# Hybrid decoder step: the first output block's gated rows prepared in the last projection round, rows loaded four halves deep, and three operations moved from GpSimd to VectorE

## The chip, the cores and the metric

The kernel runs on one core of one Trainium2 chip. The metric is the device time of one execution in microseconds (us), a median over runs. The engines are named as the profile names them: PE is TensorE's matmuls (PEld its weight loads), DVE is VectorE, ACT is ScalarE, POOL is GpSimd, and SP is the engine whose queue issues the DMAs.

## The reference, cut to what matters

Everything is float32. There are 1024 prompt rows and 8 samples of 4 rows, the model width is 1024, and there are two layers: one of sliding-window attention, then one of gated DeltaNet. The change lies nearly wholly in the second layer's output projection and in the samples' part of that layer.

```python
def modulate(x, c, norm_g, w_mod, b_mod):
    shift, scale, gate = jnp.split(jax.nn.silu(c) @ w_mod + b_mod, 3, axis=-1)
    h = rms_norm(x, norm_g) * (1 + scale[:, None]) + shift[:, None]
    return h, gate[:, None]
...
# each layer:  x <- x + gate * Branch(h);  a final rms_norm follows the last layer
# gated DeltaNet branch, per head (16 value heads of 128, chunks of 64 rows):
#   S_t = e^{g_t} S_{t-1} + k_t u_t^T
#   u_t = beta_t (v_t - (e^{g_t} S_{t-1})^T k_t),   o_t = S_t^T q_t / sqrt(dk)
#   out = (rms_norm(o) * silu(z)) @ w_out          # 2048 -> 1024
```

The samples start from states `S` that are loaded (one of 128 x 128 for each sample and head), and their new states are outputs.

## The kernel before, in words

Each fp32 matmul is made of three matmuls: an operand `x` is split into `hi` (a cast by ACT) and `lo` (a subtraction `x - hi` by DVE or POOL), and hi·hi, lo·hi and hi·lo are summed in PSUM.

The program is written out by a planner that runs when the kernel is built. Pieces of work are Python generators ("jobs"), which `weave(gen, name, hq)` hands over. A job yields a condition (`idle`, `sure`, `soon`, `over`, or a function) before it issues an instruction; the planner keeps a planned clock of each engine and picks among the waiting jobs by rank: the table `K`, in the closing stage (`nc.closing`) the table `KT`, and for the chains of head pair `hq` the table `KR`. `EX`, `TB`, `SW`, `MS` and `MM` are further numbers of the planner: margins and places. `GP` says which of five kinds of operation go to POOL instead of DVE. The engines run their instructions in the order that comes out; semaphores bind them.

On PE the program has these stages, by the time of the profiled execution: start to 74 us, attention layer to 394, its output projection to 508, DeltaNet's projections and chunk chains to 1348 (eight rounds, one for each pair of heads), and the closing stage to the end.

The closing stage multiplies the gated rows by `w_out`. `out_block(b)` makes block b of 18: part 0 (value heads 0 to 7) for eight blocks of 128 prompt rows and then the samples, and part 1 (heads 8 to 15) likewise. A block of prompt rows is 2 halves of the columns x 8 heads x 3 matmuls of 512 columns, and `pos[0]` counts 16 steps a block. Its jobs are:

- `prepare(b)` loads two halves of gated rows (`of`, 256 KB each, from the DRAM tile `gTd`), casts them (`ohi`, ACT) and subtracts (`olo`).
- `rows_of(b)` loads the rows `xt` to which the product is added.
- `gather(b)` multiplies the PSUM bank by the gate row (`y`, DVE), which frees the bank, and adds it to `xt`; `squares` and `finish` norm and store.
- `load_out` loads `w_out` in pieces of 128 x 512 (`wr`), casts them (`h2hi` or `whB`) and subtracts (`h2lo` or `wlB`).

Between the blocks' matmuls stand the last head pair's `chain` (matmuls `vo,UZ`, `uo,ks`, `S,qT`, `uo,DP`, `S,kT`), the gate row (`modG,selt`), and the samples: `states_times` multiplies the 128 loaded state tiles by the samples' queries and keys in `zq`, `core` does the recurrence, and `new_states` makes and stores the new states from `U` and `kb`.

Of the kernel before, what the change touches and what calls it, by code (L numbers as in the profile page):

```python
# [5 lines left out]
F32 = mybir.dt.float32  # L6
F32R = mybir.dt.float32r
# [7 lines left out]
P = 128  # L15
# [3 lines left out]
NB = TP // P  # L19
DB = 8  # L20
# [7 lines left out]
HQ = 8  # L28
# [214 lines left out]
def f(ap):  # L243
    return ap.bitcast(F32)
# [53 lines left out]
def body(tc, I, O, cst_ap, dbg=None):  # L298
# [19 lines left out]
    SP = (2, 20)  # L318
    AM = (3, 12)
    AT = (-5, 3)  # L320
    EX = (1.7, 2.5, 0.8, 0.7)
    ES, EN, EL, EM = EX
    K = {'split': 13, 'add': 0, 'attend': 40, 'turning': 0, 'modulate': 17, 'cached': 16, 'wo': 37, 'turn': 0, 'ahead': 2, 'taps': 2, 'gating': 5, 'decay': 23, 'samples': 38, 'load': 6, 'mod': 3, 'shape': 12, 'decays': 58, 'prepare': 58, 'gather': 8, 'finish': 10, 'states': 28, 'core': 2, 'new': 4}
    KT = {'prepare': 3, 'gather': 33, 'finish': 24, 'states': 19, 'core': 7, 'new': 14, 'load': 19, 'gating': 6, 'samples': 5, 'output': 23}
    KR = [{'chain': 4, 'output': 15, 'solve': 5, 'invert': 18, 'blocks': 40, 'decayed': 22}, {'chain': 31, 'output': 31, 'solve': 12, 'invert': 31, 'blocks': 39, 'decayed': 37}, {'chain': 9, 'output': 2, 'solve': 29, 'invert': 41, 'blocks': 1, 'decayed': 11}, {'chain': 23, 'output': 23, 'solve': 4, 'invert': 4, 'blocks': 0, 'decayed': 23}, {'chain': 10, 'output': 2, 'solve': 45, 'invert': 40, 'blocks': 1, 'decayed': 56}, {'chain': 8, 'output': 15, 'solve': 6, 'invert': 16, 'blocks': 49, 'decayed': 12}, {'chain': 0, 'output': 1, 'solve': 11, 'invert': 20, 'blocks': 34, 'decayed': 14}, {'chain': 10, 'output': 2, 'solve': 45, 'invert': 28, 'blocks': 1, 'decayed': 56}]
    TB = (3, 0)
    SW = (35, 1)
    MS = (39, 13)
    AH, AI = (a / 10 for a in AM)
    GP = (0, 1, 1, 1, 1)  # L330
    ORD = ['zzkv', 'zqzvk', 'zqzkv', 'qzzvk', 'qzzkv', 'vqzzk', 'qzzkv', 'qvzz']
    MM = (7, 12)
    ORDER = [("q", 2), ("q", 3), ("q", 4), ("q", 5), ("z", 0), ("k", 1), ("z", 1), ("z", 2), ("q", 6), ("q", 7),
             ("z", 3), ("z", 4), ("z", 5), ("z", 6), ("z", 7)]
    SE = ("vector", "vector", "vector", "vector")
# [213 lines left out]
    def over(*names):  # L549
        return lambda: not any(e[2] in names for e in jobs)  # L550
# [1333 lines left out]
    if True:  # L1884
# [446 lines left out]
        def load_out(*cuts):  # L2331
# [14 lines left out]
            while raws_:  # L2346
# [9 lines left out]
                loaded.add((k, hf))  # L2356
                fetch()

        def start():
            w_raw(0)  # L2360
            for q in range(2):
                yield idle("scalar", w_raw.tiles[0][q])
                w_split(0, q)
# [16 lines left out]
        for r in range(HQ):  # L2380
            if r > 0:
                weave(chain(r - 1, states.pop(r - 1)), "chain", r - 1)
                weave(decayed(r, states[r]), "decayed", r)
            pz = [2 * r, 2 * r + 1]
            for what in ORD[r]:
                if what in "kv" and r + 1 < HQ and r + 1 not in states:
                    states[r + 1] = {}
                    weave(decay_blocks(r + 1, states[r + 1]), "decay")
                    weave(solve(r + 1, states[r + 1]), "solve", r + 1)
                if what == "q":  # L2390
                    proj_kq(r, states[r], (1,))
                elif what == "z":
                    proj_z(pz.pop(0))
                elif what == "k":
                    until(lambda: finished[0] >= r - 1)
                    proj_kq(r + 1, states[r + 1], (0,))
                else:
                    until(lambda: gs is not None and gated[0] >= 4 * (r - 1))
                    proj_v(r, states[r])
                    if r + 1 == HQ:  # L2400
                        weave(chain(r, states.pop(r)), "chain", r)
# [11 lines left out]
        nc.parts |= {x2d.tensor.name, gTd.tensor.name}  # L2413
        gate = x3.tile([P, D], F32, name="gp", tag="gp")

        pos, prepared, stored, opened, gathered, outs = [0], {}, [0], [], [-1], [0]

        def prepare(b, part, t):

            cs = slice(t * P, (t + 1) * P)  # L2420
            ohl = prepared[b] = []
            if t == NB:
                yield over("core")
            for kk in range(2):
                if t == NB:
                    yield lambda: pos[0] >= 16 * (b - 1) + 8 + 8 * kk
                    gh = x3.tile([P, 4, P], F32R, tag="ohi", name="ohi", bufs=2)
                    g4 = gsT[:, HK * part + 4 * kk:HK * part + 4 * kk + 4]
                    yield idle("scalar", g4)
                    nc.scalar.copy(gh[:, :, 0:TS], g4)  # L2430
                    yield idle("vector", gh)
                    nc.vector.tensor_sub(gh[:, :, TS:2 * TS], g4, f(gh[:, :, 0:TS]))
                    ohl.append((gh,))
                    continue
                yield lambda: b == 0 or len(prepared[b - 1]) > kk
                r0 = part * HK + 4 * kk
                of = x3.tile([P, 4, P], F32, tag="of", name="of", bufs=2)
                nc.sync.dma_start(of, gTd[t, :, r0:r0 + 4])
                yield lambda: pos[0] >= 16 * (b - 1) + 8 + 8 * kk
                ohi = x3.tile([P, 4, P], F32R, tag="ohi", name="ohi", bufs=2)  # L2440
# [8 lines left out]
        xts_ = {}  # L2449

        def rows_of(b, part, t):
            yield lambda: stored[0] >= b - 1 - (b > NB)
            cs = slice(t * P, min((t + 1) * P, T))
            if b > NB and b % 3 == 0:
                xt = xts_[b] = hp.tile([P, D], F32, tag="h2lo2", name="xt")
            else:
                xt = xts_[b] = x3.tile([P, D], F32, tag="xt", name="xt", bufs=2)
            nc.sync.dma_start(xt[0:cs.stop - cs.start], (x2d if part else x1d)[cs])
# [80 lines left out]
        def out_block(b):  # L2539

            part, t = blocks_[b]
            for i in (0, 1) if b == 0 else (b + 1,):
                if i <= LB:
                    weave(prepare(i, *blocks_[i]), "prepare")
# [85 lines left out]
            convolved[half] = acc  # L2630

        def states_times():
            zq = sg.tile([P, DB, HQ, 32], F32, name="zq")
            yield from samples(0)
            qk = convolved[0].rearrange("p (i h) t -> p h i t", i=2)
            weave(samples(1), "samples")
# [13 lines left out]
            for b in range(DB):  # L2650
                yield idle("gpsimd")
                nc.gpsimd.memset(zq[:, b], 0.0)
            for b in range(DB):
                c0 = 8 * (b % 4)
                yield idle("vector", qk)
                nc.vector.tensor_copy(zq[:, b, :, c0:c0 + 8].rearrange("p h (i t) -> p h i t", i=2),
                                      qk[:, :, :, b * DS:(b + 1) * DS])
            ahead = 0
            for n in range(SB):
                if n == SB // 2:  # L2660
# [2 lines left out]
            for u in range(0, len(us_), 2):  # L2663
                b, hd, _ = us_[u]
                if u % 16 == 0:
                    yield over("chain", "output")
                    pk = yield from bank("mi")
                yield lambda: pos[0] >= SW[0] + SW[1] * (u + 1) / 10
                yield sure(ES, sts[u], sts[u + 1], zq)
                for j in range(4):  # L2670
                    nc.tensor.matmul(pk[32 * j:32 * j + 32, hd * 256:(hd + 1) * 256], zq[:, b, 4 * hd + j, :],
                                     sts[u + j // 2][:, 2 * (j % 2):2 * (j % 2) + 2, :].rearrange("p h d -> p (h d)"),
                                     start=(b % 4 == 0), stop=(b % 4 == 3), skip_group_check=True)
# [363 lines left out]
```

## Time and profile before

| what | value |
|---|---|
| median of 3 runs | 1617.11 us (1614.87 to 1619.9) |
| the profiled execution's own time | 1616.25 us |
| its span, first to last instruction | 1614.5 us |
| mean granted TensorE clock | 0.997 |
| PE busy | 1579.1 us |
| DVE busy | 1203.3 us |
| ACT busy | 843.1 us |
| POOL busy | 209.9 us |

The busy times are those of the span. In the profile's lines, `L84` is a helper that records nearly every operation, so instructions are told apart by their tiles: `ps_pj<-h2hi,olo` is the matmul that writes PSUM tile `ps_pj` from `h2hi` and `olo`. A line of waits has the engine and its tile, then the engine and the tile that it waited for, then total, count and the longest in us.

### The profile page before, as it was taken

How to read it: one execution, taken by the hardware profiler on the slowest of the kernel's cores; microseconds unless marked ns; L12 is line 12 of the kernel's file. 1: busy time of each engine (PE TensorE's matmuls, PEld its weight loads, DVE VectorE, ACT ScalarE, POOL GpSimd, SP SyncE). 2: the span in 40 equal slices, each digit the busy share in tenths (PEclk: the TensorE clock that was granted, in tenths of full speed). 3: DMA queues.
4: the chain of work that ended last, by engine and by line, in shares of the span. 5: the costliest groups of instructions: out<-in, count | busy, mean ns of one | idle time of the engine just before them, and what ended most of it. 6: DMA issues, size and time to landing. Idle time of an engine off the chain costs nothing. (4 is left out here: it accounts for less than half of the span.)

```text
span 1614.5 us, 30776 instructions
## 1 busy us (share of the span) xinstructions
PE 1579.1 (98%) x10714; PEld 1404.6 (87%) x10714; DVE 1203.3 (75%) x3781; ACT 843.1 (52%) x2422; POOL 209.9 (13%) x284
## 2 busy tenths in 40 slices
PE   9999999999999999999999999999999998999997
PEld 7888888987778999989999999999999997767775
DVE  6737677665665788897988769798688887757777
ACT  4635555444344655566564655665466465423332
POOL 1300000000223002020020000201001013233323
PEclk9999999999999999999999999999999999999999
DMA  9442220115343333233333324324243136675884
GB/s 365 153 140 79 79 81 28 40 47 154 103 146 108 98 93 81 81 92 91 105 70 90 100 58 128 72 62 121 65 126 80 46 102 206 202 263 178 289 270 158
DMA packets 178826, 195.70 MB, mean 121 GB/s; under 512 B 76848, under 2 KB 120720, under 8 KB 178640
## 3 DMA queue, kind: packets, MB, share of 16 engines
q1 hardware_dynamic: 178672, 193.75, 40.1%
q8 instruction: 84, 1.38, 0.4%
q14 instruction: 70, 0.57, 0.1%
HBM read 146.45 MB, written 49.27 MB: 121 GB/s over the span
## 5 line engine op out<-in xcount | busy, mean ns | idle before, releaser
L84 PE MATMUL ps_pj<-h2lo,wh 128*128 128x384 f32 (+1 forms) x1128 | 377.3, 335 | 0.0
L84 PE MATMUL ps_pj<-h2hi,wl 128*128 128x384 f32 (+1 forms) x1128 | 377.2, 334 | 0.0
L84 PE MATMUL ps_pj<-h2hi,wh 128*128 128x384 f32 (+1 forms) x1128 | 375.6, 333 | 0.0
L84 PEld LDWEIGHTS ps_pj<-h2lo,wh 128*128 128x128 f32 x1128 | 212.8, 189 | 2.1
L84 PEld LDWEIGHTS ps_pj<-h2hi,wh 128*128 128x128 f32 x1128 | 212.7, 189 | 2.1
L84 PEld LDWEIGHTS ps_pj<-h2hi,wl 128*128 128x128 f32 x1128 | 212.8, 189 | 1.5
L84 POOL TENSOR_TENSOR Xd<-Xc,cst 32x128 f32<-32x128 f32 x128 | 66.3, 518 | 459.7 <-DMA Xc<-Xdd 247.6
L84 PE MATMUL ps_pj<-hhi,wh 128*128 128x384 f32 (+1 forms) x376 | 123.9, 331 | 0.5 <-ACT hhi L84 0.4
L84 PE MATMUL ps_pj<-hlo,wh 128*128 128x384 f32 (+1 forms) x376 | 123.4, 331 | 0.1
L84 PE MATMUL ps_pj<-hhi,wl 128*128 128x384 f32 (+1 forms) x376 | 122.2, 328 | 0.0
L84 DVE SCALAR_TENSOR_TENSOR vT<-XR,cT,vT 128x384 f32<-128x384 f32 (+1 forms) x144 | 83.1, 582 | 13.4 <-ACT vT L84 12.2
L84 DVE TENSOR_TENSOR wl<-wr,wh 128x512 fp32r<-128x512 f32 x120 | 83.6, 696 | 11.7 <-ACT wh L84 10.5
L84 ACT CAST wh<-wr 128x512 fp32r<-128x512 f32 x128 | 78.5, 615 | 20.7 <-PE ps_pj L84 19.4
L84 POOL TENSOR_TENSOR xt<-xt,y 128x512 f32<-128x512 f32 (+1 forms) x47 | 64.2, 1370 | 184.2 <-DVE y L84 165.6
L84 PEld LDWEIGHTS ps_pj<-hlo,wh 128*128 128x128 f32 x376 | 70.6, 188 | 7.2 <-issue 6.2
L84 PEld LDWEIGHTS ps_pj<-hhi,wh 128*128 128x128 f32 x376 | 70.5, 188 | 6.8 <-issue 4.7
L84 PEld LDWEIGHTS ps_pj<-hhi,wl 128*128 128x128 f32 x376 | 70.6, 188 | 4.2 <-issue 4.2
L84 ACT COPY XR<-ps_pj 128x384 f32<-128x384 f32 (+1 forms) x96 | 43.2, 450 | 56.4 <-PE ps_pj L84 56.2
L84 ACT ACTIVATE qe<-ps_mi,Eg 128x128 f32<-128x128 f32 x112 | 35.0, 364 | 68.4 <-PE ps_mi L84 65.0
L84 ACT ACTIVATE prob<-prob,nm 128x256 f32<-128x256 f32 (+1 forms) x128 | 62.3, 489 | 15.5 <-DVE nm L84 15.4
L84 DVE TENSOR_TENSOR X<-X,tmp 128x126 f32<-128x126 f32 (+22 forms) x248 | 63.7, 257 | 8.5
L84 DVE TENSOR_TENSOR tmp<-X 128x126 f32<-128x126 f32 (+22 forms) x248 | 62.5, 252 | 7.6 <-POOL X L84 3.3
(555 smaller groups left out, 3858.2 us busy)
## 6 DMA issues: line engine op xcount, KB each, us to landing
wr<-in_gwb SPq DMA_DIRECT2D x96, 256.0 KB
S<-in_states SPq DMA_DIRECT2D x42, 256.0 KB
wm<-in_wm SPq DMA_DIRECT2D x16, 512.0 KB
wr<-in_winb SPq DMA_DIRECT2D x32, 256.0 KB
wmod<-in_w_mod SPq DMA_DIRECT2D x32, 256.0 KB
wm<-in_w_mod SPq DMA_DIRECT2D x32, 256.0 KB
DP<-gcr SPq DMA_DIRECT2D x64, 128.0 KB
zl<-zd SPq DMA_DIRECT2D x32, 256.0 KB
```

Of the source, the lines that this page charges most:

```text
L84: inst = fn(*args, **kwargs)
```

## The change

Six things are edited.

1. `early()` is new. It is woven in the last round, ahead of the projection of `v`, and does for block 0 what `prepare(0)` did: two loads of gated rows, two casts on ACT and two subtractions on DVE, here in place, so that `of` becomes the low part. The tiles lie in four slots of the projections' pool `kwp`. `out_block(0)` weaves no `prepare(0)` any more.
2. `prepare(b)` issues both loads at once, into four buffers `of` instead of two, and doesn't wait for the block before to have made its half. `rows_of` waits in addition until `pos[0]` is 2 (block 0) or 14 (later ones).
3. `zq` holds four samples instead of eight. Four fills on POOL instead of eight; samples 4 to 7 are placed by four DVE copies when the first half of the products has been issued.
4. `GP` sends three kinds of operation to DVE instead of POOL: every second split in `load_out`, the second `olo` of a block, and the additions `xt<-xt,y`. That is 62 operations of 128 x 512: 16, 16 and 30.
5. The planner's numbers `EX`, `K`, `KT`, `KR`, `TB`, `SW`, `MS` and `MM` are others, so the order of instructions is another.
6. The number of instructions is the same on PE, ACT and SP; DVE has 62 more, POOL 66 fewer.

```diff
-    EX = (1.7, 2.5, 0.8, 0.7)
+    EX = (1.2, 1.6, 0, 0.9)
...
-    KT = {'prepare': 3, 'gather': 33, 'finish': 24, 'states': 19, 'core': 7, 'new': 14, 'load': 19, 'gating': 6, 'samples': 5, 'output': 23}
+    KT = {'prepare': 3, 'gather': 20, 'finish': 40, 'states': 15, 'core': 7, 'new': 9, 'load': 19, 'gating': 5, 'samples': 40, 'output': 22}
...
-    GP = (0, 1, 1, 1, 1)
+    GP = (0, 0, 0, 1, 0)
...
+        first_rows = []
+        def early():
+            kwp_ = Watched(nc, kwp)
+            raws = []
+            for kk in range(2):
+                of, ohi = (kwp_.tile([P, 4, P], F32R, tag="t2", name=nm, bufs=4) for nm in ("of", "ohi"))
+                nc.sync.dma_start(f(of), gTd[0, :, 4 * kk:4 * kk + 4])
+                raws.append((of, ohi))
+            for of, ohi in raws:
+                yield idle("scalar", of)
+                nc.scalar.copy(ohi, f(of))
+                yield idle("vector", ohi)
+                nc.vector.tensor_sub(of, f(of), f(ohi))
+                first_rows.append((ohi, of))
...
+                    if r + 1 == HQ:
+                        weave(early(), "prepare")
                     proj_v(r, states[r])
...
-        pos, prepared, ... = [0], {}, ...
+        pos, prepared, ... = [0], {0: first_rows}, ...
         def prepare(b, part, t):
-            cs = slice(t * P, (t + 1) * P)
             ohl = prepared[b] = []
+            ofs = []
+            for kk in range(2 * (t < NB)):
+                r0 = part * HK + 4 * kk
+                of = x3.tile([P, 4, P], F32, tag="of", name="of", bufs=4)
+                nc.sync.dma_start(of, gTd[t, :, r0:r0 + 4])
+                ofs.append(of)
...
-                yield lambda: b == 0 or len(prepared[b - 1]) > kk
-                r0 = part * HK + 4 * kk
-                of = x3.tile([P, 4, P], F32, tag="of", name="of", bufs=2)
-                nc.sync.dma_start(of, gTd[t, :, r0:r0 + 4])
+                of = ofs[kk]
...
         def rows_of(b, part, t):
-            yield lambda: stored[0] >= b - 1 - (b > NB)
+            yield lambda: stored[0] >= b - 1 - (b > NB) and pos[0] >= (2, 14)[b > 0]
...
-            zq = sg.tile([P, DB, HQ, 32], F32, name="zq")
+            zq = sg.tile([P, 4, HQ, 32], F32, name="zq")
...
                 if u % 16 == 0:
+                    if u:
+                        for i in range(4, DB):
+                            yield from place(i)
```

How this moves instructions is seen in the order on each engine. First PE, where the last projection (`ps_pj<-h2hi,wl`) and the first output matmuls (`ps_pj<-h2hi,ohi`) stand. `uo`, `vo`, `S` and `ks` belong to the last head pair's chain. Before:

```order
L84 MATMUL ps_pj<-h2lo,wh 128x288
L84 MATMUL ps_pj<-h2hi,wl 128x288
L84 MATMUL ps_mi<-uo,ks 128x128 x2
L84 MATMUL ps_mi<-S,qT 128x256
L84 MATMUL ps_mi<-uo,DP 128x128 x2
L84 MATMUL ps_mi<-S,kT 128x256
L84 MATMUL ps_ob<-vo,UZ 128x128 x2
L84 MATMUL ps_mi<-uo,ks 128x128 x2
L84 MATMUL ps_mi<-S,qT 128x256
L84 MATMUL ps_mi<-uo,DP 128x128 x2
L84 MATMUL ps_lg<-modG,selt 128x512
```

Three rows later the first output matmul follows. Now:

```order
L84 MATMUL ps_ob<-vo,UZ 128x128 x2
L84 MATMUL ps_pj<-h2hi,wh 128x288
L84 MATMUL ps_pj<-h2lo,wh 128x288
L84 MATMUL ps_pj<-h2hi,wl 128x288
L84 MATMUL ps_pj<-h2hi,ohi 128x512
L84 MATMUL ps_pj<-h2hi,of 128x512
L84 MATMUL ps_mi<-uo,ks 128x128 x2
L84 MATMUL ps_pj<-h2lo,ohi 128x512
L84 MATMUL ps_mi<-S,qT 128x256
L84 MATMUL ps_mi<-uo,DP 128x128 x2
L84 MATMUL ps_pj<-h2hi,ohi 128x512
```

The first block's matmuls now follow the last projection at once, and the chain's steps stand among them. At one place of that block, after 33 of its 48 matmuls, the order still has two steps of the chain side by side:

```order
L84 MATMUL ps_pj<-h2hi,of 128x512
L84 MATMUL ps_pj<-h2lo,ohi 128x512
L84 MATMUL ps_ob<-vo,UZ 128x128 x2
L84 MATMUL ps_mi<-uo,ks 128x128 x2
L84 MATMUL ps_mi<-S,qT 128x256
L84 MATMUL ps_mi<-uo,DP 128x128 x2
L84 MATMUL ps_pj<-h2hi,ohi 128x512
```

The second place is on DVE, around 1462 to 1472 us of the profile before, where the samples' `U` is made (four steps, one after the other with ACT) and then their outputs `oH`. Before:

```order
L84 TENSOR_TENSOR y<-ps_tr,gp 128x512
L84 TENSOR_TENSOR U_17924<-ps_lg,U_17924 32x512
L84 TENSOR_TENSOR y<-ps_ob,gp 128x512
L84 TENSOR_TENSOR U_17924<-ps_lg,U_17924 32x512 x3
L84 TENSOR_SCALAR oH<-KQ,egH 128x128
L84 SCALAR_TENSOR_TENSOR oH<-VH,cQ,oH 128x128
L84 TENSOR_SCALAR oH<-oH,rkq 128x128
L84 TENSOR_SCALAR oH<-KQ,egH 128x128
L84 SCALAR_TENSOR_TENSOR oH<-VH,cQ,oH 128x128 x2
L84 TENSOR_SCALAR oH<-oH,rkq 128x128
L84 TENSOR_TENSOR olo<-of,ohi 128x512
```

Now:

```order
L84 TENSOR_TENSOR U_17920<-ps_lg,U_17920 32x512
L84 TENSOR_TENSOR y<-ps_ob,gp 128x512
L84 TENSOR_TENSOR U_17920<-ps_lg,U_17920 32x512
L84 TENSOR_TENSOR xt<-xt,y 128x512
L84 TENSOR_TENSOR U_17920<-ps_lg,U_17920 32x512
L84 TENSOR_SCALAR oH<-KQ,egH 128x128
L84 SCALAR_TENSOR_TENSOR oH<-VH,cQ,oH 128x128
L84 TENSOR_SCALAR oH<-oH,rkq 128x128
L84 TENSOR_SCALAR oH<-KQ,egH 128x128
L84 SCALAR_TENSOR_TENSOR oH<-VH,cQ,oH 128x128
L84 TENSOR_TENSOR olo<-of,ohi 128x512 x2
L84 SCALAR_TENSOR_TENSOR oH<-VH,cQ,oH 128x128
```

Both `olo` of the block stand on DVE now, one `oH` step sooner than the one did, and the additions `xt<-xt,y`, which POOL made, lie between the steps of `U`.

More of the change, by code (lines that the diff above doesn't have):

```diff
@@ L320, in body @@
     AT = (-5, 3)
-    EX = (1.7, 2.5, 0.8, 0.7)
+    EX = (1.2, 1.6, 0, 0.9)
     ES, EN, EL, EM = EX
-    K = {'split': 13, 'add': 0, 'attend': 40, 'turning': 0, 'modulate': 17, 'cached': 16, 'wo': 37, 'turn': 0, 'ahead': 2, 'taps': 2, 'gating': 5, 'decay': 23, 'samples': 38, 'load': 6, 'mod': 3, 'shape': 12, 'decays': 58, 'prepare': 58, 'gather': 8, 'finish': 10, 'states': 28, 'core': 2, 'new': 4}
-    KT = {'prepare': 3, 'gather': 33, 'finish': 24, 'states': 19, 'core': 7, 'new': 14, 'load': 19, 'gating': 6, 'samples': 5, 'output': 23}
@@ L325, in body @@
-    KR = [{'chain': 4, 'output': 15, 'solve': 5, 'invert': 18, 'blocks': 40, 'decayed': 22}, {'chain': 31, 'output': 31, 'solve': 12, 'invert': 31, 'blocks': 39, 'decayed': 37}, {'chain': 9, 'output': 2, 'solve': 29, 'invert': 41, 'blocks': 1, 'decayed': 11}, {'chain': 23, 'output': 23, 'solve': 4, 'invert': 4, 'blocks': 0, 'decayed': 23}, {'chain': 10, 'output': 2, 'solve': 45, 'invert': 40, 'blocks': 1, 'decayed': 56}, {'chain': 8, 'output': 15, 'solve': 6, 'invert': 16, 'blocks': 49, 'decayed': 12}, {'chain': 0, 'output': 1, 'solve': 11, 'invert': 20, 'blocks': 34, 'decayed': 14}, {'chain': 10, 'output': 2, 'solve': 45, 'invert': 28, 'blocks': 1, 'decayed': 56}]
@@ L326, in body @@
-    TB = (3, 0)
-    SW = (35, 1)
-    MS = (39, 13)
+    K = {'split': 6, 'add': 9, 'attend': 22, 'turning': 24, 'modulate': 20, 'cached': 7, 'wo': 36, 'turn': 0, 'ahead': 2, 'taps': 2, 'gating': 6, 'decay': 23, 'samples': 28, 'load': 6, 'mod': 35, 'shape': 12, 'decays': 22, 'prepare': 60, 'gather': 23, 'finish': 19, 'states': 40, 'core': 37, 'new': 7}
+    KT = {'prepare': 3, 'gather': 20, 'finish': 40, 'states': 15, 'core': 7, 'new': 9, 'load': 19, 'gating': 5, 'samples': 40, 'output': 22}
+    KR = [{'chain': 4, 'output': 15, 'solve': 5, 'invert': 18, 'blocks': 44, 'decayed': 22}, {'chain': 31, 'output': 31, 'solve': 13, 'invert': 31, 'blocks': 39, 'decayed': 37}, {'chain': 32, 'output': 2, 'solve': 30, 'invert': 41, 'blocks': 1, 'decayed': 11}, {'chain': 23, 'output': 38, 'solve': 4, 'invert': 4, 'blocks': 0, 'decayed': 23}, {'chain': 9, 'output': 2, 'solve': 23, 'invert': 44, 'blocks': 1, 'decayed': 58}, {'chain': 8, 'output': 36, 'solve': 8, 'invert': 12, 'blocks': 58, 'decayed': 12}, {'chain': 8, 'output': 15, 'solve': 8, 'invert': 12, 'blocks': 58, 'decayed': 12}, {'chain': 10, 'output': 0, 'solve': 42, 'invert': 28, 'blocks': 1, 'decayed': 56}]
@@ L329, in body @@
+    TB = (3, 2)
+    SW = (22, 3)
+    MS = (57, 8)
     AH, AI = (a / 10 for a in AM)
-    GP = (0, 1, 1, 1, 1)
+    GP = (0, 0, 0, 1, 0)
     ORD = ['zzkv', 'zqzvk', 'zqzkv', 'qzzvk', 'qzzkv', 'vqzzk', 'qzzkv', 'qvzz']
-    MM = (7, 12)
+    MM = (11, 4)
     ORDER = [("q", 2), ("q", 3), ("q", 4), ("q", 5), ("z", 0), ("k", 1), ("z", 1), ("z", 2), ("q", 6), ("q", 7),
@@ L2414, in body @@
         gate = x3.tile([P, D], F32, name="gp", tag="gp")
-        pos, prepared, stored, opened, gathered, outs = [0], {}, [0], [], [-1], [0]
+        pos, prepared, stored, opened, gathered, outs = [0], {0: first_rows}, [0], [], [-1], [0]
         def prepare(b, part, t):
-            cs = slice(t * P, (t + 1) * P)
             ohl = prepared[b] = []
+            ofs = []
[4 more added lines that the diff above has]
+                ofs.append(of)
             if t == NB:
@@ L2543, in out_block @@
                 if i <= LB:
-                    weave(prepare(i, *blocks_[i]), "prepare")
+                    if i:
+                        weave(prepare(i, *blocks_[i]), "prepare")
                     weave(rows_of(i, *blocks_[i]), "prepare")
@@ L2648, in fetch, with place @@
                     sts.append(st)
-            for b in range(DB):
+            for b in range(4):
                 yield idle("gpsimd")
                 nc.gpsimd.memset(zq[:, b], 0.0)
-            for b in range(DB):
+            def place(b):
                 c0 = 8 * (b % 4)
                 yield idle("vector", qk)
-                nc.vector.tensor_copy(zq[:, b, :, c0:c0 + 8].rearrange("p h (i t) -> p h i t", i=2),
+                nc.vector.tensor_copy(zq[:, b % 4, :, c0:c0 + 8].rearrange("p h (i t) -> p h i t", i=2),
                                       qk[:, :, :, b * DS:(b + 1) * DS])
+            for b in range(4):
+                yield from place(b)
             ahead = 0
@@ L2670, in states_times @@
                 for j in range(4):
-                    nc.tensor.matmul(pk[32 * j:32 * j + 32, hd * 256:(hd + 1) * 256], zq[:, b, 4 * hd + j, :],
+                    nc.tensor.matmul(pk[32 * j:32 * j + 32, hd * 256:(hd + 1) * 256], zq[:, b % 4, 4 * hd + j, :],
                                      sts[u + j // 2][:, 2 * (j % 2):2 * (j % 2) + 2, :].rearrange("p h d -> p (h d)"),
```

## The prediction

> **What bounds the kernel now.** I read first the page's busy times, since a stage whose engine is full needs no further search.
>
> ```profile
> PE 1579.1 (98%) x10714; PEld 1404.6 (87%) x10714; DVE 1203.3 (75%) x3781; ACT 843.1 (52%) x2422; POOL 209.9 (13%) x284
> ```
>
> TensorE is busy for 1579.1 of 1614.5 us, so at most 35.4 us of the span are not matmuls, and the change neither adds nor drops a matmul. What it can win are waits of PE. The profiled execution took 1616.25 us: the span and 1.75 us around it. The median of the runs shown, 1617.11, lies 0.86 above it; the sum below is made against 1616.25.
>
> Second, the waits of PE in the closing stage and the 18 us ahead of it (1330 to 1615 us), where nearly all of the change lies: what was waited for, total us, times, longest.
>
> ```profile
> PE ps_pj L84 <- ACT ohi L84: 1.6, 2, 0.9
> PE ps_mi L84 <- ACT uo L84: 1.6, 2, 1.1
> PE ps_pj L84 <- DVE y L84: 1.3, 2, 0.9
> PE ps_pj L84 <- DVE ohi L84: 1.1, 1, 1.1
> PE ps_mi L84 <- ACT kb L84: 1.1, 1, 1.1
> PE ps_pj L84 <- POOL olo L84: 1.0, 1, 1.0
> PE ps_ob L84 <- DVE UZ L84: 0.7, 1, 0.7
> PE ps_lg L84 <- DVE UZ L84: 0.6, 1, 0.6
> PE ps_mi L84 <- DVE S L84: 0.6, 1, 0.6
> PE ps_ob L84 <- DVE vo L84: 0.4, 1, 0.4
> PE ps_pj L84 <- DVE olo L84: 0.2, 1, 0.2
> ```
>
> These eleven rows come to 10.2 us: all that the closing stage can give by plain waits. Ahead of 1330 us the two orders hold the same matmuls, with whole stretches equal word for word; where they differ, the matmuls between a producer and its consumer are about as many. I cost that part at nothing, within 1 us either way (at stake is one wait of the size of those in this table, in round 3, where a chain comes earlier and some cover is gone).
>
> Third, the place where the chain of the last head pair runs alone, as PE's timeline (start, us, instruction, idle before it), and one row of ACT.
>
> ```profile
> 1347.90 0.29 PE L84 MATMUL ps_pj<-h2hi,wl 128*128 128x288 f32 x1
> 1350.66 0.75 PE L84 MATMUL ps_ob<-vo,UZ 128*128 128x128 f32 x4 [0.45 <-DVE vo L84]
> 1352.46 0.71 PE L84 MATMUL ps_mi<-uo,ks 128*128 128x128 f32 x4 [1.05 <-ACT uo L84]
> 1356.94 0.49 PE L84 MATMUL ps_pj<-h2hi,ohi 128*128 128x512 f32 x1 [0.73 <-ACT ohi L84]
> 1357.66 0.50 PE L84 MATMUL ps_pj<-h2hi,olo 128*128 128x512 f32 x1 [0.23 <-DVE olo L84]
> ...
> 1367.58 0.71 PE L84 MATMUL ps_mi<-uo,ks 128*128 128x128 f32 x4 [0.56 <-ACT uo L84]
> 1376.46 0.51 PE L84 MATMUL ps_pj<-h2hi,ohi 128*128 128x512 f32 x1 [0.93 <-DVE y L84]
> 1380.91 0.67 PE L84 MATMUL ps_mi<-S,kT 128*128 128x256 f32 x2 [0.56 <-DVE S L84]
> ```
>
> ```profile
> 1356.27 0.62 ACT L84 CAST ohi<-of 128x512 fp32r<-128x512 f32 x1 [1.55 <-DMA of<-gTd]
> ```
>
> The last projection ends at 1347.90; the first output matmul comes 9 us later, because its rows come late: ACT's cast stood 1.55 us for their DMA.
>
> Fourth, a place where two waits are followed by a slower clock (timeline, then windows: us, busy and count of each engine, granted clock).
>
> ```profile
> 1469.20 0.50 PE L84 MATMUL ps_pj<-h2hi,ohi 128*128 128x512 f32 x1 [0.88 <-ACT ohi L84]
> 1470.69 0.50 PE L84 MATMUL ps_pj<-h2hi,olo 128*128 128x512 f32 x1 [0.99 <-POOL olo L84]
> ```
>
> ```profile
> 1471.40:1474.80 3.40, 3.40 (x10) 2.63 (x9) 3.22 (x9) 0.00 (x0) 0.55 (x1) 0.50 0.55 116
> 1475.00:1481.00 6.00, 6.00 (x29) 4.99 (x28) 4.35 (x12) 1.03 (x2) 1.29 (x1) 1.00 0.17 60
> ```
>
> The counts hold records that only reach into a window, two or three each. Eight starts in 3.40 us at clock 0.50 are one every 0.425 us, 26 in 6.00 us at 1.00 one every 0.23, so this stretch lost 8 x 0.195 = 1.6 us: the price of the two waits over and above their 1.87 us.
>
> **The change, part by part.** *The first block's rows beside the last projections.* The early part issues two DMAs, two ACT casts and two DVE subtractions in the last round, instead of the same six ahead of the first block; none is added, two DMAs of SP's queue come earlier. In the new order the first block's matmuls follow the last projection directly, and the chain's steps lie between them. The five waits from 0.45 to 0.56 in the timeline (0.45 + 1.05 + 0.73 + 0.23 + 0.56 = 3.02 us) lose their reason. Each of them also makes the first matmul after it start alone; from one start to the next, the stretch to 1382 us stands idle for some 6.4 us, an estimate from the starts and ends in the timeline, against 4.51 us in the list (the five, 0.93 and 0.56). What stays: block 1 still waits for the bank that DVE's `y` frees, 0.93 us; and one pair of chain steps (`vo,UZ`, then `uo,ks`) still stands with nothing between, which cost 1.05 us + the copy's start here, about 1.4. So 6.4 - 0.9 - 1.4 = 4.1, taken as 4 us. Its ends are 0 (the weights' split on DVE, not the rows, is what comes last: three more such splits stand ahead of the chain's `vo`) and 6.4.
>
> *The steps at 1336 us.* The two waits for `UZ` (0.7 and 0.6) now have more projection matmuls ahead of them in the order. I take 0.8 of 1.3 us; the ends are 0 and 1.3.
>
> *Rows four halves deep.* Both halves of a block are asked for at its start. The queue of SP shows what that removes:
>
> ```profile
> SPq L84 <- POOL olo L84: 33.4, 11, 6.4
> ```
>
> 33.4 us of SP's waiting in 11 times, for a buffer that POOL still reads. The queue has stores of `xt` and loads of states behind it. No wait of PE in the table above is for `of` or for a store, so I take 0; if it were the cause of the late cast at 1468.5 us it would be one 0.88 us wait, which the next item counts already.
>
> *Work from POOL to DVE.* The durations, by groups in 1340 to 1615 us (busy us, mean ns), and two rows of DVE with nothing of POOL beside them:
>
> ```profile
> L84 POOL TENSOR_TENSOR xt<-xt,y 128x512 f32<-128x512 f32 x30 | 39.7, 1330 | 88.0 <-DVE y L84 81.3 <-DMA of<-gTd 2.9 <-DVE sv L84 2.4
> L84 POOL TENSOR_TENSOR olo<-of,ohi 128x512 fp32r<-128x512 f32 x16 | 22.1, 1383 | 45.3 <-ACT ohi L84 40.0 <-DMA S1w<-in_states 3.3 <-issue 1.8
> L84 DVE TENSOR_TENSOR olo<-of,ohi 128x512 fp32r<-128x512 f32 x16 | 12.1, 757 | 15.6 <-ACT ohi L84 15.6
> L84 DVE TENSOR_SCALAR ks<-ktok,sd 128x128 f32<-128x128 f32 x16 | 6.3, 507 | 4.1 <-PE ps_mi L84 4.1
> ```
>
> ```profile
> 1355.09 0.28 DVE L84 TENSOR_SCALAR ks<-ktok,sd 128x128 f32<-128x128 f32 x1
> 1356.91 0.69 DVE L84 TENSOR_TENSOR olo<-of,ohi 128x512 fp32r<-128x512 f32 x1 [1.55 <-ACT ohi L84]
> ```
>
> In all 62 operations of 128x512 go to DVE: 30 `xt`, 16 `olo` and 16 splits of weights. POOL took about 1.35 us for one, DVE takes 0.69: 62 x 0.69 = 42.8 us more of DVE. Its free time in the stage:
>
> ```profile
> 1350.00:1400.00 50.00, 45.10 (x237) 34.93 (x236) 39.48 (x100) 25.62 (x79) 15.75 (x19) 1.00 0.62 199
> 1400.00:1450.00 50.00, 49.83 (x295) 31.51 (x295) 29.83 (x87) 16.92 (x39) 12.35 (x10) 1.00 0.84 276
> 1450.00:1500.00 50.00, 46.63 (x213) 35.34 (x212) 40.57 (x91) 18.91 (x38) 19.64 (x15) 0.97 0.57 185
> 1500.00:1550.00 50.00, 48.93 (x224) 39.56 (x223) 35.83 (x104) 15.98 (x38) 17.11 (x13) 1.00 0.91 307
> 1550.00:1600.00 50.00, 50.00 (x227) 39.87 (x226) 38.80 (x112) 18.82 (x43) 17.77 (x14) 1.00 0.60 194
> ```
>
> DVE (third) sums to 184.5 of 250 us. With all 42.8 on top it is 227.3, 91%; the fullest stretch, 1450 to 1500, would stand at 40.57 + 8.6 = 49.2 of 50. Against this stands that DVE's own operations now take longer beside POOL's: `ks` 507 ns on average and 280 alone, `olo` 757 and 690. Sixteen of each return 16 x 0.227 + 16 x 0.067 = 4.7 us; with the others of such shapes I estimate up to 23 us, hence between 82% and 91%. DVE stays off the bound, and an `olo` or `xt` comes 0.7 us sooner than from POOL when DVE is free.
>
> The Trainium skill, "SBUF — State Buffer", section "SBUF: two separate sides", says that VectorE's second pair of ports and GpSimd share access under a lock held for the whole instruction; the stretched `ks` and `olo` agree with it, and if the lock were all, the move would cost DVE 42.8 less what it gets back. Its "Perfetto Trace Analysis", section "Optimizing Scalar/DVE Operations", speaks against the change: where DVE is saturated, offloading to GpSimd may make sense, and here work goes the other way; by that rule the time would be that of the third rival, and at 74% busy the trace does not yet call DVE saturated.
>
> *The waits from 1455 to 1520 us.* At 1470.69 PE waited 0.99 us for POOL's `olo`; DVE makes it in 0.69 instead of 1.4 us, but behind `oH` steps. The wait of 0.88 ahead of it is for ACT, held by casts of `U`, and the order keeps that. I take 0.9 for `olo`, and 1.6 for the clock, since the second of the two waits then shrinks: 2.5 us. The ends are -4.3 (both waits and the clock go, plus the 1.1 of `kb` partly) and +1 (nothing goes, `olo` comes later than from POOL). The other waits of 1.1 each (`ohi` of the samples, `kb`) stay.
>
> The Trainium skill, "TensorE: Matmul & The Clock Gate", section "What's actually happening", has half the clock after a whole idle window of about 3.4 us; in this trace 1.87 us of waits in 2.4 us (1468.32 to 1470.69) were enough, and by the page's rule alone there would have been no slow stretch to win back, which takes 1.6 off the sum: 1612 us.
>
> *The samples' queries in half the room.* Four fills of POOL go (0.3 us each) and four copies of DVE wait for the first half of the states' products to be done. PE's first state product after them waits for at most four short DVE copies, estimated at 0.3 us each from the 0.28 us of a 128x128 row: 1.2 us, if no out block's matmul is left to lie between. I take 0, because the loop puts other blocks' matmuls there, and keep +1.2 as an end.
>
> *Other ranks.* DVE's new place in the order costs something that no row shows: with 62 more operations some bank or half of rows will come late once. I add 1 us, between 0 and 12 (18 blocks at 0.7 us each, one operation late in each).
>
> *The end.* Behind the last matmul stands the same tail:
>
> ```profile
> 1605.20 0.69 DVE L84 TENSOR_TENSOR y<-ps_ob,gp 128x512 f32<-128x512 f32 x1
> 1610.24 0.81 SPq L84 DMA_DIRECT2D out_y_p<-xt  x2
> ```
>
> From 1605.20 to 1614.5 are 9.3 us of final norm and store, and their instructions stay: 0, within 0.3.
>
> **Sum.** 1616.25 - 4 - 0.8 - 2.5 + 1 = 1609.95, with 0.5 left for round 3: 1610.5 us.
>
> **The rivals.** *The waits only move.* The first block stands for the last weights or for banks, one wait is exchanged for another, and what remains is 0 to 1 us: 1615.5 us. For it speaks that the weights' splits share DVE with the chain and that 0.93 us for the bank stays; against it that the row of ACT shows rows, not weights, as last. *Nearly all goes.* The 10.2 us, 1.6 of clock and 1.9 of lone starts, less 0.9 for a bank: 12.8, hence 1603.5 us. Against it: `kb` and the samples' `ohi` wait for steps whose order is kept. *DVE becomes the bound.* Where DVE passes about 95% busy in a 50-us window, `y` frees its bank late in every block; 18 x 0.7 = 12 us of waits against 5 won: 1623 us. For it speaks 49.2 of 50; against it the stretched operations that shrink.
>
> **How the numbers follow.** A measurement of this kernel tells about 0.3% from no change: 4.85 us, so faster begins below 1612.3 and slower above 1622.0. Forecast (1608 to 1612.3) 0.46, nearly all 0.10, waits only move (1612.3 to 1617.5) 0.33, DVE the bound 0.11. Faster is 0.46 + 0.10 = 0.56; the third rival between 1617.5 and 1622 goes to same: 0.35; slower 0.09. The range 1604.5 to 1617.5 leaves out DVE as the bound and half of the best case, under 2 in 10.
>
> **What would show it.** Right: no wait for `ohi` or `uo` between the last projection and the first block, and the first `ohi` matmul within 1 us of that projection; no window of clock 0.50 near 1470 us; POOL at some 125 us, 8% (209.9 less 62 x 1.35 and the fills); DVE at 82 to 91% from 1350 to 1600 us; no SP wait for POOL's `olo`. Wrong: PE waits for `h2lo`, `wlB` or `y` on DVE in most blocks, or new waits in the rounds ahead of 1330 us.

## The result and the profile after

The changed kernel takes 1603.65 us (median of 4 runs, 1601.69 to 1607.26) against 1617.12 us before (4 runs, 1614.87 to 1619.9): the ratio is 0.9918, with a 95% interval of 0.9895 to 0.9942. It is faster, as forecast, but by 13.5 us where 6.6 were forecast, and the time lies 0.85 us below the lower end of the range. So the forecast was wrong in size. The time is that of the second rival ("nearly all goes", 1603.5 us), but its mechanism came only in part: 4.5 us of the listed waits stayed, and 1.8 us came from the tail, which no rival counted.

The page's busy times of the changed kernel:

```profile
PE 1574.7 (98%) x10714; PEld 1402.9 (88%) x10714; DVE 1213.6 (76%) x3843; ACT 841.9 (53%) x2422; POOL 126.1 (8%) x218
```

PE's waits from 1330 to 1605 us, where the prediction listed eleven rows:

```profile
PE ps_pj L84 <- DVE y L84: 1.6, 2, 0.9
PE ps_mi L84 <- ACT kb L84: 1.0, 1, 1.0
PE ps_pj L84 <- ACT ohi L84: 0.7, 1, 0.7
PE ps_mi L84 <- ACT uo L84: 0.5, 1, 0.5
PE ps_pj L84 <- DVE olo L84: 0.5, 1, 0.5
PE ps_pj L84 <- DVE h2lo L84: 0.2, 1, 0.2
```

10.2 us have become 4.5. (The view of before has two more rows than the prediction listed, 0.3 us for `U` and 0.2 for a state, 10.7 in all; both are gone.) Left are the bank that `y` frees, now in two blocks, one `kb`, one `ohi` and the one uncovered pair of chain steps.

PE's timeline shows the first place. The first output matmul starts 0.13 us after the last projection does, where it was 9.04:

```profile
1345.81 0.29 PE L84 MATMUL ps_pj<-h2hi,wl 128*128 128x288 f32 x1
1345.94 0.40 PE L84 MATMUL ps_pj<-h2hi,ohi 128*128 128x512 f32 x1
...
1361.01 0.71 PE L84 MATMUL ps_mi<-uo,ks 128*128 128x128 f32 x4 [0.52 <-ACT uo L84]
...
1367.65 0.47 PE L84 MATMUL ps_pj<-h2hi,ohi 128*128 128x512 f32 x1 [0.71 <-DVE y L84]
...
1374.30 0.50 PE L84 MATMUL ps_pj<-h2hi,ohi 128*128 128x512 f32 x1 [0.88 <-DVE y L84]
```

The place of the slow clock, with the window behind it (busy us and count of each engine, granted clock):

```profile
1461.88 0.50 PE L84 MATMUL ps_pj<-h2hi,ohi 128*128 128x512 f32 x1 [0.67 <-ACT ohi L84]
1462.85 0.50 PE L84 MATMUL ps_pj<-h2hi,olo 128*128 128x512 f32 x1 [0.46 <-DVE olo L84]
```

```profile
1461.90:1465.30 3.40, 2.94 (x13) 2.24 (x14) 3.29 (x10) 1.37 (x3) 0.00 (x0) 1.00 0.47 119
```

Both waits are still there, but they come to 1.13 us instead of 1.87, and the clock stays at 1.00.

DVE's groups in the closing stage and the window of 250 us that answers to the five of before:

```profile
L84 DVE TENSOR_TENSOR olo<-of,ohi 128x512 fp32r<-128x512 f32 x30 | 20.5, 687 | 11.9 <-ACT ohi L84 11.3 <-DMA S<-in_states 0.5
L84 DVE TENSOR_SCALAR ks<-ktok,sd 128x128 f32<-128x128 f32 x16 | 3.9, 278 | 2.8 <-PE ps_mi L84 2.8
```

```profile
1340.00:1590.00 250.00, 245.31 (x1261) 187.70 (x1260) 203.66 (x572) 98.16 (x238) 3.64 (x6) 1.00 0.72 237
```

In these windows DVE rose from 184.5 to 203.7 of 250 us, 81.5%; they do not hold quite the same work, as the later one begins ahead of the last projection. Over the whole program the page has 1213.6 us instead of 1203.3, 10.3 more, where the 62 operations alone come to 42.8: some 32 us came back. Operations that were stretched beside POOL's are so no more: `olo` takes 687 ns on average instead of 757, and `ks` 278 instead of 507.

The tail, which I had put at nothing, is the third place. Before (PE's last output matmul, then DVE):

```profile
1602.69 0.40 PE L84 MATMUL ps_ob<-h2lo,ohi 128*128 128x512 f32 x1
1602.89 1.12 DVE L84 SCALAR_TENSOR_TENSOR S1w<-S1w,gtb,ps_mi 128x128 f32<-128x128 f32 x4 [0.28 <-PE ps_mi L84]
1603.93 0.75 DVE L84 SCALAR_TENSOR_TENSOR xt<-xt,rs,fng 128x512 f32<-128x512 f32 x1
1604.60 0.69 DVE L84 TENSOR_TENSOR xt<-xt,y 128x512 f32<-128x512 f32 x1
```

After:

```profile
1592.06 1.41 DVE L84 SCALAR_TENSOR_TENSOR xt<-xt,rs,fng 128x512 f32<-128x512 f32 x2
...
1592.43 0.39 PE L84 MATMUL ps_ob<-h2lo,ohi 128*128 128x512 f32 x1
...
1593.39 0.68 DVE L84 TENSOR_TENSOR y<-ps_ob,gp 128x512 f32<-128x512 f32 x1
```

Before, the last `y` started at 1605.20, 2.51 us after the last output matmul, because new-state steps (`S1w`) and two `xt` steps stood ahead of it on DVE. Now it starts 0.96 us after, with `xt` steps alone ahead of it.

Where the 12.0 us between the two profiled spans lie, worked out from PE's starts at places where both programs have issued about as many matmuls (within 6). The matmuls ahead of such a place are not all the same ones, so a single row is good to about 1 us:

| stretch (time before) | before, us | after, us | difference | forecast |
|---|---|---|---|---|
| start to 1327.5 | 1327.5 | 1327.0 | -0.5 | +0.5 |
| to 1338.0 (`UZ`) | 10.5 | 8.8 | -1.7 | -0.8 |
| to block 4, 1428.6 | 90.6 | 85.1 | -5.5 | -4 |
| to block 6, 1461.1 | 32.5 | 33.6 | +1.1 | part of +1 |
| to block 8, 1491.3 | 30.2 | 26.1 | -4.1 | -2.5 |
| to the last output matmul, 1602.7 | 111.4 | 111.8 | +0.5 | part of +1 |
| to the end | 11.8 | 10.0 | -1.8 | 0 |

### The profile page after: what moved, and what is told of

Its sections match the earlier page's. It is cut to its first block, busy times and chain, and to the rows that moved or that the text cites. A ratio compares the mean times of both kernels' runs of the same rounds, so it can differ in the third digit from the quotient of the medians.

```text
span 1602.4 us, 30728 instructions
## 1 busy us (share of the span) xinstructions
PE 1574.7 (98%) x10714; PEld 1402.9 (88%) x10714; DVE 1213.6 (76%) x3843; ACT 841.9 (53%) x2422; POOL 126.1 (8%) x218
## 5 line engine op out<-in xcount | busy, mean ns | idle before, releaser
L84 PE MATMUL ps_pj<-h2hi,ohi 128*128 128x512 f32 (+1 forms) x136 | 55.6, 409 | 2.3 <-DVE y L84 1.6
```

The lines of the kernel that those rows point to most:

```text
L84: inst = fn(*args, **kwargs)
```

## The experiments

In four runs the engine of an operation is changed without the planner knowing of it; in the others a part of the change is taken out or done alone, and the planner orders anew unless the text says otherwise. Where an order is kept, that holds for PE and ACT; the order in which SP issues DMAs moves in places all the same. Times are medians; the ratio is to runs of the kernel before that were made beside them (medians 1616.01 to 1617.11 us).

**Engines alone, in the order of the changed kernel.** The planner still counts the operations on DVE, so PE's and ACT's orders stay the same; only the issue goes to POOL. It is 61 operations here: the second subtraction of block 0 is `early()`'s and stays on DVE.

```diff
+nc.real = "gpsimd" if <k % 2, kk, or n < 2 * LB> else None
 getattr(nc, eng).tensor_sub(...)          # the splits, olo, xt
+nc.real = None
```

> The changed kernel with its order kept word for word on PE and ACT, but the 62 operations (weights' splits, second olo, xt additions) issued on POOL again. Theory A (the order and the early rows carry most, DVE's share is the stretch 1454 to 1480 us where olo and the samples' rows come sooner): 4 us come back, 1607 to 1609 us, with PE waiting for POOL's olo again near 1462 us. Rival B (it is the faster engine, not the order): at least 8 of the 13 us come back, 1612 us or more. Rival C (the engine is indifferent): 1603 to 1605 us.

Measured 1610.09 us, ratio 0.9953 (0.9941 to 0.9966): 6.4 us slower than the change, between the 4 of theory A and the 8 of rival B. In the trace the closing stage is 2.8 us longer and the tail 0.3; another 2.7 us lie ahead of everything that was changed (below). PE's waits in the stage:

```profile
PE ps_mi L83 <- DVE S L83: 2.0, 2, 1.4
PE ps_lg L83 <- DVE oH L83: 1.3, 1, 1.3
...
PE ps_pj L83 <- POOL olo L83: 1.0, 1, 1.0
```

The wait for POOL's `olo` is back, and DVE's own steps (`S`, `oH`) come late as well. DVE's operations are stretched again: those `olo` that it still makes take 924 ns on average, and `ks` 474.

**Engines alone, in the order of the kernel before.** The same edit the other way round.

> The kernel before with its order kept on PE and ACT, but the 62 operations issued on DVE. Theory A: the waits for POOL's olo and the half clock at 1471 us go, 3 us, so 1613 to 1615 us; the waits between 1350 and 1357 us stay. Rival B: 8 us or more faster, below 1609 us. Rival C: 1616 to 1618 us.

Measured 1616.15 us, ratio 0.9994 (0.9981 to 1.0006): no change, as rival C had it. By its trace the closing stage became 0.8 us shorter and the tail 0.45. The half clock at 1471 us was gone, but PE then stood 1.86 us for the samples' `ohi` (1489.46), where it had stood 1.14. In the old order the faster engine is worth about 1 us by the trace and nothing clear by the medians; expected were 3.

**The early rows alone.** `early()` and the empty `prepare(0)` in the kernel before.

> The kernel before with the early rows of block 0 alone (old ranks, POOL as before, the planner orders anew). Theory A: the first block runs beside the chain, 5 us faster, 1611 to 1613 us. Rival B: within 2 us of before. Rival D (only the new ranks put the chain's steps where they are covered): within 2 us of before, with uo and vo waits still there.

Measured 1613.51 us, ratio 0.9978 (0.9966 to 0.9991), 3.6 us faster, 0.5 us outside what theory A expected. From 1327 us to the middle of block 0 it had won 4.4 us (1.5 of them at `UZ`), where 4.8 were estimated; then part went into new waits (block 1's bank, the samples' rows):

```profile
1370.61 0.50 PE L84 MATMUL ps_pj<-h2hi,ohi 128*128 128x512 f32 x1 [1.08 <-DVE y L84]
...
1485.70 0.69 PE L84 MATMUL ps_pj<-h2hi,ohi 128*64 128x512 f32 x1 [3.45 <-DVE ohi L84]
```

**The changed kernel without the early rows.**

> The changed kernel without the early rows: block 0 is prepared when the first block opens, as before. Theory A: 5 us slower than the change, 1608 to 1610 us, with the waits for vo, uo and ohi back after the last projection. Rivals B and D: within 2 us of the change, 1602 to 1606 us.

Measured 1621.05 us, ratio 1.0026 (1.0015 to 1.0037): 17.4 us slower than the change and slower than before. Some 4 us of it lie in the first block, as expected. The larger part lies elsewhere:

```profile
1469.46 0.71 PE L84 MATMUL ps_lg<-erl,oH 128*128 128x128 f32 x4 [4.00 <-DVE oH L84]
...
1471.69 0.80 PE L84 MATMUL ps_mi<-U,kb 96*128 96x256 f32 x2 [1.08 <-ACT kb L84]
1474.66 0.79 PE L84 MATMUL ps_pj<-h2hi,ohi 128*128 128x512 f32 x1 [2.17 <-DVE y L84]
```

The order that the planner writes without `early()` turns the samples' outputs `oH` too soon. Between the start of the last `uT` step and that turning, PE has 10.9 us of other work here and 15.4 in the changed kernel, while DVE needs about 15 for the steps between. Behind the first of these waits the granted clock was 0.50 from 1469.87 to 1480.11 us, so it cost more than its length. I had expected only the first part.

**Code and numbers apart.** First the changed code with the old numbers, then the old code with the new numbers.

> The changed code (early rows, four buffers, half zq, the 62 operations on DVE) with the old planner's numbers. Theory A2 (the parts need each other: early rows alone gave 3.6 us, DVE alone about 1, and the new ranks place the samples' and the chain's steps for that code): the sum of the single parts, 1611 to 1614 us. Rival D2 (the code carries it, the numbers are a detail): 1603 to 1607 us.

Measured 1614.38 us, ratio 0.9992 (0.9981 to 1.0003): 0.4 us above what theory A2 expected, and no clear change.

> The code before with the new planner's numbers alone. Theory A2: no faster than before, 1617 to 1625 us, because the changed kernel without its early rows already stood at 1621. Rival D3 (the numbers carry the change): 1603 to 1610 us.

Measured 1639.37 us, ratio 1.0134 (1.0117 to 1.0151), 14 us beyond the upper end expected. PE waits 6.68 us for `oH` at 1483.66, with 9.3 us of other work ahead of it. So the code alone is worth 0 to 3 us, the numbers alone cost 22, and both together win 13.5. Neither carries the change; the numbers fit this code.

**Two buffers of rows instead of four**, the order of PE, ACT, DVE and POOL kept. Both loads of a block are still asked for at once, so this is not the loading of the kernel before.

> The changed kernel with two buffers of rows instead of four, every engine's order word for word the same. The prediction's step (SP's wait for of is hidden): 1602 to 1606 us, as the change. Rival E: rows come late again, ACT's casts wait for DMA, 3 us or more slower, 1607 us or above.

Measured 1607.6 us, ratio 0.9951 (0.9936 to 0.9965), 4 us slower than the change. By the trace 2.2 us are in the closing stage, and 4.7 lie ahead of it, where both programs have the same instructions; so the 2.2 are what the buffers can be held to. DVE's and PE's timelines show it, first DVE:

```profile
1505.24 0.69 DVE L84 TENSOR_TENSOR olo<-of,ohi 128x512 fp32r<-128x512 f32 x1 [2.35 <-ACT ohi L84]
1505.85 0.34 DVE L84 SCALAR_TENSOR_TENSOR S<-S,gtb,ps_mi 128x128 f32<-128x128 f32 x1
1506.11 0.68 DVE L84 TENSOR_TENSOR h2lo<-wr,h2hi 128x512 fp32r<-128x512 f32 x1
```

```profile
1506.84 0.50 PE L84 MATMUL ps_ob<-h2lo,ohi 128*128 128x512 f32 x1 [2.04 <-DVE h2lo L84]
```

DVE stood 2.35 us for a cast whose rows came late; the split of the weights, which PE needed at that moment, stood behind it in DVE's queue. Rival E was right in direction, and at its lower end by the medians; the price is that of another operand than the late one.

**`zq` for eight samples, with two buffers** (as much room as before; the order is another).

> The changed kernel with zq for eight samples and two buffers of rows (as much room as before; the planner orders anew). Theory A2: zq itself is worth nothing, so as the run with two buffers, within 2 us of it. Rival F (the four late copies of DVE cost PE a wait, or the early ones do): 3 us or more away from it.

Measured 1619.68 us, ratio 1.0025 (1.0015 to 1.0035), 12 us slower than with two buffers alone. PE waits 4.24 us for `oH` at 1474.05, with 11.0 us of other work ahead. No wait for `zq` itself shows; it is the order again. The distance is that of rival F, but not for its reason, and what `zq` alone is worth stays open.

**The rows early, the order kept** up to the first block: in the kernel before, only the two loads are issued in the last round.

> The kernel before with the loads of block 0's rows issued in the last round, while casts, subtractions and the order up to the first block stay as they were (behind the first block the order differs in places). Theory A (what was lost after the last projection is the chain without matmuls between, and only the order mends it): the cast's wait for DMA goes, but the first output matmul still starts at least 7 us after the last projection; 0 to 1.5 us gained there. Rival G (the late rows were the price): 4 us gained there, the first output matmul within 5 us of the last projection.

```profile
1347.38 0.29 PE L84 MATMUL ps_pj<-h2hi,wl 128*128 128x288 f32 x1
...
1350.14 0.75 PE L84 MATMUL ps_ob<-vo,UZ 128*128 128x128 f32 x4 [0.44 <-DVE vo L84]
1351.65 0.71 PE L84 MATMUL ps_mi<-uo,ks 128*128 128x128 f32 x4 [0.77 <-ACT uo L84]
...
1353.77 1.13 PE L84 MATMUL ps_lg<-modG,selt 128*128 128x512 f32 x2 [0.53 <-DMA selt<-in_cst]
...
1354.98 0.58 PE L84 MATMUL ps_pj<-h2hi,ohi 128*128 128x512 f32 x1
```

From the last projection to the first output matmul it is 7.6 us, where it was 9.04: loading the rows early won 1.4 us (a new wait of 0.53 for another load included), and the rest is the chain with no matmuls between its steps, as theory A had it. The whole run took 1624.07 us, ratio 1.0051 (1.0038 to 1.0065), because of later waits in an order that changed behind the first block (3.91 us for `kb` at 1522.98).

**The tail**: the new `EX` alone in the kernel before.

> The kernel before with the new EX alone (the planner's margins). At the end of DVE's order no new-state step (S1w) stands ahead of the last y any more. Theory A: the stretch from the last output matmul's start to the end falls from 11.8 to about 10 us, as in every run with the new numbers. Rival H (the tail's length comes from elsewhere, POOL or the stores): it stays at 11.3 to 12.

```profile
1615.86 0.39 PE L84 MATMUL ps_ob<-h2lo,ohi 128*128 128x512 f32 x1
1616.29 0.69 DVE L84 TENSOR_TENSOR y<-ps_ob,gp 128x512 f32<-128x512 f32 x1
```

From the last output matmul to the end of the span, 1625.6, it is 9.7 us, against 11.8, as theory A had it: no `S1w` step stands between the last output matmul and the last `y` any more, which starts 0.43 us after it. All runs with the new numbers have 8.9 to 10.3 us there, all with the old `EX` 11.2 to 15.3. The run itself took 1627.01 us, ratio 1.0066 (1.0055 to 1.0078), with 4.23 us of waiting for `oH` at 1484.84.

**One kind of operation on POOL at a time**, in the order of the changed kernel: the `olo` (15, without block 0's), then the additions. The splits of weights alone were not run.

> The changed kernel, order kept on PE and ACT, with the 16 olo on POOL alone. Theory A: olo is what PE waits for, so most of what all 62 cost in the closing stage (3 us by the traces) is here: 1606 to 1608 us. Rival I (the additions or the splits are what matters): 1603 to 1605 us.

Measured 1606.51 us, ratio 0.9941 (0.9929 to 0.9954), as theory A expected; 2.2 us in the closing stage by the trace.

> The changed kernel, order kept on PE and ACT, with the 30 additions xt on POOL alone. Theory A: nobody on PE waits for xt, DVE gets 20 us back: 1602 to 1605 us. Rival I: POOL's additions stretch DVE's operations beside them, the samples' oH come later and PE waits for them: 1606 us or more.

Measured 1612.69 us, ratio 0.9979 (0.9969 to 0.999). My theory failed here: the additions alone cost more than all three kinds together, 7.4 us in the closing stage by the trace. SP's waits (1380 to 1512 us, then 1500 to 1503.5), then DVE's and PE's timelines:

```profile
SPq L83 <- POOL xt L83: 19.1, 5, 7.2
```

```profile
SPq L83 <- DMA out_new_s_s<-S: 4.3, 1, 4.3
```

```profile
1508.03 0.86 DVE L83 SCALAR_TENSOR_TENSOR S<-S,gtb,ps_mi 128x128 f32<-128x128 f32 x3 [2.92 <-DMA S<-in_states]
...
1509.67 0.69 DVE L83 TENSOR_TENSOR h2lo<-wr,h2hi 128x512 fp32r<-128x512 f32 x1
```

```profile
1510.41 0.50 PE L83 MATMUL ps_ob<-h2lo,ohi 128*128 128x512 f32 x1 [3.19 <-DVE h2lo L83]
```

DVE waits for a state, and the split of the weights that PE needs stands behind that in DVE's queue. The last load of a state ahead of this was issued at 1503.21 only: SP first waited 4.3 us for the store of an earlier state, and the load stands later in SP's queue than in the changed kernel, behind the loads of weights. Rival I's time came, but not its reason: no wait for `oH` shows. SP's 19.1 us for POOL's `xt` lie ahead of this, the last of them before 1490 us; what part they have in it was not shown. With all three kinds on POOL, every second split leaves DVE's queue, and this wait is not in that run's list.

## Why the prediction was wrong, and where it was right

The direction and the mechanism of the two main parts were right; the sum was not. Between the two traces 12.0 us were won where the sum has 5.8. The 6.2 us between lie in the tail (1.8 against 0), the stretch of `olo` and the clock (1.6 more than forecast), the first block (1.5 more), the start (1.0) and `UZ` (0.9), less 0.6 that other ranks gave back beyond the 1 forecast. The step that failed by its own bounds is the tail, put at "0, within 0.3" and measured at 1.8 us; the second is "the other waits of 1.1 each stay", of which one went. The range was also cut above the second rival's own time, 1603.5 us.

- *The first block beside the chain* (-4, ends 0 and -6.4): right in mechanism, with one reason wrong. The first output matmul did not come 9 us late "because its rows come late": with only the loads early it came 7.6 us late, so the rows were 1.4 us of it and the bare chain the rest. The stretch to block 4 gave 5.5 us, that to block 6 4.4, near the forecast; the run with the early rows alone had won 2.9 by the middle of block 0. The two waits that were to stay, the bank and the one pair of steps, stayed (0.71, 0.88 and 0.52 us).
- *`UZ`* (-0.8, ends 0 and -1.3): under-sized. Both waits went, 1.3 us, and the stretch gave 1.7.
- *`olo` and the clock* (-2.5, ends -4.3 and +1): right in mechanism, under-sized; the stretch gave 4.1. The step that failed is "the other waits of 1.1 each stay": `kb` stayed (0.97), but that for the samples' `ohi` (1.14 at 1491.34) is gone. It stood at 1.86, 3.45 and 2.77 us in the runs with DVE alone, the early rows alone and the loads early, all in the old code with the old numbers. It was absent with the changed code under the old numbers, and in the old code with the new numbers or the new `EX` alone, where PE had stood 4 to 7 us for `oH` before it; so several parts bear on it, and which one removes it stays open.
- *The tail* (0, within 0.3): wrong, 1.8 us. The step counted from the last `y` on, although `y` itself stood behind other steps on DVE; it should have counted from the last output matmul. The run with the new `EX` alone shows the cause: with no `S1w` step ahead of `y` the tail is 9.7 us.
- *Four buffers* (0): the reason given was not enough. The 33.4 us of SP's waiting were dismissed because PE had no wait "for `of` or for a store"; but a late row holds DVE, and PE then waits for the weights behind it, which in the changed order costs some 2 us by the trace. In the kernel before PE had no such wait, so what the buffers won over it is not shown. SP's waiting is not gone either: it is 18.7 us now, in 8 times, for DVE's `olo`.
- *Other ranks* (+1, between 0 and 12): the rows with 1.1 and 0.5 us are near it, but that they are a price of the ranks was not shown. The numbers are no part that can be priced alone: they cost 22 us with the old code.
- *DVE as the bound* did not come: 81.5%, just under the 82 to 91% forecast. The "up to 23 us" that DVE would get back had no sum behind it. The Trainium skill, "Perfetto Trace Analysis", section "Optimizing Scalar/DVE Operations", warns that moving work between GpSimd and VectorE might not help because they share a port. Here 42.8 us of operations moved back and DVE's busy time rose by 10.3, and with them on POOL again `ks` went from 278 to 474 ns, which agrees with a shared port; in the changed order the move paid, in the old one hardly.

Of the seven stretches five came out shorter than forecast, and the two terms put at zero (tail and buffers) had not been followed through the queue of the engine between. The start, 1.0 us of the difference, is within what executions differ by anyway (below): that part is chance.

## What to carry to other kernels

Measure the tail from the last matmul, and read the order of the engine behind it: each step ahead of the last one counts in full. When an operand is late, look at what stands behind its consumer in that engine's queue, and not only at who waits for it by name. A set of ranks belongs to its code: with one part taken out, an otherwise good order waited 4 to 7 us at a place that the part does not touch, so the cover of each long chain (here 15 us for `oH`) is worth checking after every edit.

## What the runs showed of the hardware

Whether the clock falls behind a wait does not follow from the wait's length. Behind a single wait of 2.04 us (two buffers, 1506.84) it fell; behind one of 1.69 us with another of 0.64 soon after (without the early rows, 1518.87 and 1520.97) it fell; behind a single wait of 2.77 us (only the loads early, 1492.27) it stayed at 1.00.

In the traces the granted clock is 0.50 for 3.41 us or a whole multiple of that (but for one that reaches the end of a trace), and within one trace all such stretches begin on one grid of 3.41 us. Cut on the edges of that grid, PE's busy time (the first figure behind the length) tells the cases apart. Granted clock third from the end; first two buffers, then only the loads early, then the kernel before:

```profile
1504.61:1508.02 3.41, 1.37 (x6) 1.01 (x6) 2.75 (x5) 1.63 (x3) 0.00 (x0) 1.00 1.00 369
1508.02:1511.43 3.41, 3.41 (x10) 2.63 (x9) 2.65 (x5) 0.66 (x3) 0.00 (x0) 0.50 0.86 262
```

```profile
1487.28:1490.69 3.41, 2.23 (x12) 1.68 (x10) 3.41 (x8) 0.00 (x0) 2.81 (x3) 1.00 0.79 258
1490.69:1494.10 3.41, 1.83 (x8) 1.16 (x9) 3.41 (x7) 1.31 (x4) 2.68 (x2) 1.00 0.82 250
1494.10:1497.51 3.41, 3.41 (x18) 2.27 (x18) 2.16 (x7) 1.76 (x4) 1.06 (x1) 1.00 0.67 203
```

```profile
1468.00:1471.41 3.41, 1.54 (x6) 0.82 (x5) 3.23 (x7) 3.08 (x6) 2.16 (x2) 1.00 0.84 286
1471.41:1474.82 3.41, 3.41 (x10) 2.64 (x9) 3.23 (x9) 0.00 (x0) 0.54 (x1) 0.50 0.55 116
```

The wait of 2.77 us fell across an edge and left PE busy for 2.23 and 1.83 us on its two sides; the 0.88 and 0.99 us of the kernel before fell into one stretch. From 1300 us on, in all fourteen traces, every stretch at full clock in which PE was busy for at most 1.70 us was followed by one at 0.50, except one of 1.50 us (only the loads early, from 1412.19), and none with 1.77 us or more was. Ahead of 1300 us this does not explain every case (in three traces the clock fell near 535 us behind a full stretch). The Trainium skill, "TensorE: Matmul & The Clock Gate", section "What's actually happening", names a whole idle window of about 3.4 us; the runs show that less is enough.

Executions of one program also differ ahead of everything that was changed: between the changed kernel and its variants with the same order, the start of PE's 300th matmul lay between 41.6 and 44.4 us. So medians of 4 to 12 runs differ by some us more or less than the stages of two traces do.
